# Add and GELU on one core: HBM blocks dealt to partitions in a different order

## Chip, cores and metric

The kernel runs on one core of one Trainium2 chip. The metric is device time in microseconds (us), from three runs before the change. The profile is one execution of the program, recorded by the hardware profiler; its times count from the first instruction.

## What is computed

Two float32 matrices of 1024 x 4096 are added, and the tanh form of GELU is applied to each element of the sum:

```python
def reference(x, y):                      # both float32 [1024, 4096]
    z = x + y
    return (0.5 * z * (1 + np.tanh(np.sqrt(2 / np.pi) * (z + 0.044715 * z ** 3)))).astype(np.float32)
```

Each input and the output has 16.78 MB, so 33.55 MB are read from HBM (the chip's main memory) and 16.78 MB written. Nothing is reused: each element is read once, worked on and written once.

## The kernel before

SBUF, the on-chip memory, has 128 partitions. Each of the three HBM tensors is seen as 128 blocks of 8 rows, a block being 32768 contiguous elements or 128 KB. Block p belongs to partition p. The views `xv`, `yv` and `ov` express this in one line (L93):

```python
xv, yv, ov = (a.rearrange("(p n) d -> p (n d)", p=P) for a in (x, y, out))
```

A tile `z` holds all 32768 elements of every partition. x is loaded straight into it, y into one of two buffers of 8192 elements per partition, and the sum goes back into `z`, as does the result. Columns are cut in three ways:

- loads: four pieces of 8192 columns, each of x (`load_x`, L128) and of y (`load_y`, L135). A load piece is 32 KB in each partition, 4.19 MB in all.
- computing: sixteen chunks of 2048 columns.
- stores: three pieces of 16384, 10240 and 6144 columns (`store`, L139).

For each chunk, GpSimd (POOL in the profile) adds y to x (`add`, L152; chunk 0 is added by VectorE, DVE); ScalarE (ACT) squares with a scale into a PSUM tile (`sq`, L157); VectorE forms (w + c1) * z (`stt`, L163); ScalarE takes the sigmoid (`sig`, L168); and VectorE multiplies it by z, back into `z` (`mul`, L175). The form z * sigmoid(...) equals the tanh form.

The order on each engine's queue is written out by hand at the end of the function. SyncE (SP) issues all eleven transfers on one queue: x0, y0, x1, y1, x2, y2, x3, y3, then the three stores. The issue of y2 waits until the adds on y0 are done, since they share a buffer, and y3 likewise for y1. The first store is made to wait for the first half of the multiply of chunk 9 (`FIRST`), so that it joins the queue when the loads are nearly through. Two helpers work on the compiled program: `begin_early` moves the first two loads ahead of the program's opening barrier, and `wait_late` moves the wait for the last store behind the closing barrier. The transfer hardware has 16 DMA engines; one transfer is spread over them.

## Time and profile before

| | |
|---|---|
| median of three runs | 120.35 us (120.22 to 120.42) |
| the profiled execution: its time | 120.44 us |
| the profiled execution: span, first to last instruction | 118.8 us |
| DMA queue, share of 16 engines over the span | 98.8% |
| read and written | 33.55 MB and 16.78 MB, 424 GB/s on average |
| DVE, POOL, ACT busy | 73.7, 69.6 and 61.0 us |
| x load, issue to landing (median of four) | 31.4 us |
| y load, issue to landing (median of four) | 22.2 us |
| the three stores, issue to landing | 22.0, 15.8 and 11.9 us |

The time is measured from outside and is 1.6 us longer than the span. "Busy" counts an engine's own instructions; the rest of its span it waits. For transfers, time from issue to landing includes waiting behind earlier transfers of the queue. The page also divides the span into 40 equal slices and gives, for each, an engine's busy share as a digit in tenths, the mean share of the 16 DMA engines, and the GB/s moved. A packet is what one DMA engine moves in one go.

### The profile page before, as it was taken

Reading aid. Unit: us, or ns where it says so; the run is one execution under the profiler, and the core shown is the slowest. Engines: PE = TensorE matmul, PEld = TensorE weight load, DVE = VectorE, ACT = ScalarE, POOL = GpSimd, SP = SyncE. Lnnn points to the kernel's source line nnn. Section 1 sums busy time; section 2 is a strip of 40 time slices with the busy share of each in tenths; the row PEclk is TensorE's granted clock in tenths of the full one; section 3 lists DMA queues with packets and bytes.
Section 4 is the critical chain, followed back from the end, with each engine's and each line's share of the span. In section 5 each row is a group of like instructions: output and inputs, shape, how many; then the busy total and the mean of one; then the engine's idle time right before and its main releaser. Section 6 shows DMA issues by size and latency. Waiting matters only on the chain.

```text
span 118.8 us, 172 instructions
## 1 busy us (share of the span) xinstructions
DVE 73.7 (62%) x35; ACT 61.0 (51%) x34; POOL 69.6 (59%) x19
## 2 busy tenths in 40 slices
DVE  0000000635799995739999968999994999990000
ACT  5000000063888965197698647888839779810000
POOL 0000000699996099999959999959999990000000
DMA  7989898989999898989899898998899889999996
GB/s 243 463 386 497 353 530 353 508 375 475 408 419 463 375 508 353 519 364 508 375 430 452 386 497 353 519 541 353 353 596 463 353 353 441 441 441 441 389 406 265
DMA packets 1584, 50.33 MB, mean 424 GB/s; under 512 B 176, under 2 KB 176, under 8 KB 176
## 3 DMA queue, kind: packets, MB, share of 16 engines
q1 hardware_dynamic: 1584, 50.33, 98.8%
HBM read 33.55 MB, written 16.78 MB: 424 GB/s over the span
## 4 chain that ended last, share of the span: by engine, by line
DMA 51%; POOL 26%; POOLq 4%; DVE 4%; DVEq 2%; ACT 2%; issue 0%; SPq 0%
DMA y<-in_y_dram 51%; POOL z L152 26%; POOLq L230 4%; DVE w L163 2%; DVEq L230 2%; DVE z L175 2%; ACT w L157 2%; SPq L128 0%; POOLq L152 0%
## 5 line engine op out<-in xcount | busy, mean ns | idle before, releaser
L152 POOL TENSOR_TENSOR z<-z,y 128x2048 f32<-128x2048 f32 x15 | 69.4, 4658 | 28.3 <-DMA y<-in_y_dram 28.3
L157 ACT ACTIVATE w<-z 128x2048 f32<-128x2048 f32 x16 | 30.1, 1882 | 37.7 <-DVE z L152 21.5
L163 DVE SCALAR_TENSOR_TENSOR w<-w,z 128x2048 f32<-128x2048 f32 x16 | 36.7, 2296 | 11.3 <-ACT w L157 11.1
L175 DVE TENSOR_TENSOR z<-w,z 128x2048 f32<-128x2048 f32 (+1 forms) x17 | 35.9, 2155 | 0.0
L168 ACT ACTIVATE w<-w 128x2048 f32<-128x2048 f32 x16 | 29.7, 1855 | 4.4 <-DVE w L163 4.3
L152 DVE TENSOR_TENSOR z<-z,y 128x2048 f32<-128x2048 f32 x1 | 2.3, 2291 | 20.5 <-DMA y<-in_y_dram 20.5
L215 ACT ACT_TABLE_LOAD x1 | 1.3, 1283 | 1.3 <-PEq L247 1.3
L214 DVE MEMSET one<- 128x1 f32 x1 | 0.1, 59 | 1.3 <-PEq L247 1.3
L247 POOL MEMSET const-float32-0.0<- 128x1 f32 x1 | 0.1, 99 | 0.2 <-issue 0.2
L215 ACT ACTIVATE one<-one 128x1 f32<-128x1 f32 x1 | 0.2, 203 | 0.0
L247 POOL MEMSET const-bfloat16-1.0<- 128x1 bf16 x1 | 0.1, 101 | 0.0
L247 POOL MEMSET const-uint8-127<- 128x1 uint8 x1 | 0.1, 101 | 0.0
L247 POOL MEMSET const-float32-1.0<- 128x1 f32 x1 | 0.1, 98 | 0.0
## 6 DMA issues: line engine op xcount, KB each, us to landing
z<-in_x_dram SPq DMA_DIRECT2D x4, 4096.0 KB, 31.4
y<-in_y_dram SPq DMA_DIRECT2D x4, 4096.0 KB, 22.2
out_dram<-z SPq DMA_DIRECT2D x1, 5120.0 KB, 15.8
out_dram<-z SPq DMA_DIRECT2D x1, 3072.0 KB, 11.9
out_dram<-z SPq DMA_DIRECT2D x1, 22.0
```

Of the source, the lines that this page charges most:

```text
L152: eng.tensor_add(out=zt[:, a:b], in0=zt[:, a:b], in1=yt[s][:, o : o + b - a])
L157: nc.scalar.activation(out=wt[c], in_=zt[:, a:b], func=act.Square, scale=root)
L163: nc.vector.scalar_tensor_tensor(out=wt[c], in0=wt[c], scalar=c1, in1=zt[:, a:b], op0=alu.add, op1=alu.mult)
L168: nc.scalar.activation(out=wt[c], in_=wt[c], func=act.Sigmoid)
L175: ins = nc.vector.tensor_mul(out=zt[:, a + o : a + o + n], in0=wt[c][:, o : o + n], in1=zt[:, a + o : a + o + n],)
L214: nc.vector.memset(one, 0.0)
L215: nc.scalar.activation(out=one, in_=one, func=act.Sigmoid)
L230: tc.compile()
L247: nc = _bacc.Bacc("TRN2", target_bir_lowering=False, num_devices=1)
```

## The change

The views of x, y and the output get another order. The 128 blocks are numbered 16*j + e, with e from 0 to 15 and j from 0 to 7, and the views become three-dimensional: e first, then j, then the 32768 contiguous elements of a block. Against an SBUF tile of 128 partitions, taken in order, block 16*j + e goes to partition 8*e + j. The loads and the stores use the same view, so an element is written where it was read. [...]

```diff
-    xv, yv, ov = (a.rearrange("(p n) d -> p (n d)", p=P) for a in (x, y, out))
+    xv, yv, ov = (
+        a.rearrange("(j e n) d -> e j (n d)", j=8, e=16) for a in (x, y, out)
+    )
...
-        nc.sync.dma_start(out=zt[:, a:b], in_=xv[:, a:b])
+        nc.sync.dma_start(out=zt[:, a:b], in_=xv[:, :, a:b])
...
-        nc.sync.dma_start(out=yt[s][:, o : o + b - a], in_=yv[:, a:b])
+        nc.sync.dma_start(out=yt[s][:, o : o + b - a], in_=yv[:, :, a:b])
...
-        ins = nc.sync.dma_start(out=ov[:, a:b], in_=zt[:, a:b])
+        ins = nc.sync.dma_start(out=ov[:, :, a:b], in_=zt[:, a:b])
```

Nothing else differs: sizes, tiles, waits and the order of all queues stay.

## Prediction

> **What bounds the kernel now.** I read the page from the top: busy engines first, then the transfers, then the chain.

> ```profile
> span 118.8 us, 172 instructions
> DVE 73.7 (62%) x35; ACT 61.0 (51%) x34; POOL 69.6 (59%) x19
> ...
> DMA  7989898989999898989899898998899889999996
> ...
> q1 hardware_dynamic: 1584, 50.33, 98.8%
> HBM read 33.55 MB, written 16.78 MB: 424 GB/s over the span
> ```

> No computing engine is busy for more than 62% of the span. The single transfer queue occupies the 16 DMA engines for 98.8% of it, 117.4 us each, and its row of tenths never falls between the first slice and the last. So 118.8 us is 117.4 us of transfers plus 1.4 us around them; the first instruction issues a load at 0.00, and its first data packet starts 1.0 us later.

> The chain that ended last seems to say something else:

> ```profile
> DMA 51%; POOL 26%; POOLq 4%; DVE 4%; DVEq 2%; ACT 2%; issue 0%; SPq 0%
> ```

> It leads through the last y load (landed at 80.1) into the adds and multiplies that precede the last store, issued at 106.9. But that store takes 11.9 us to land, and its 3.15 MB need only 3.15 MB / 435 GB/s = 7.2 us. For 4.7 us it stood behind the store before it. The computing chain has 4.7 us of slack at the end; the transfers have none.

> Next, how fast each engine goes. Over two stretches (columns: length, DVE, ACT, POOL, clock, DMA share, GB/s):

> ```profile
> 20.00:40.00 20.00, 14.01 (x7) 11.72 (x7) 15.58 (x3) 1.00 1.00 431
> 40.00:60.00 20.00, 16.16 (x8) 13.10 (x8) 17.93 (x4) 1.00 1.02 437
> ```

> 431 to 437 GB/s over 16 engines is 27 GB/s each, also in the stores: the trace's packet records give 1213 ns for a 32 KB load packet (27.0 GB/s) and 912 ns for a 24 KB store packet (26.9). A packet is one partition's contiguous run. All 1024 load packets take 1211 to 1238 ns, except the first sixteen, at 1.69 to 2.20 us. Summed over all packets and divided by 16, the excess over 1213 ns per 32 KB is **0.77 us**: 0.67 in those first packets, 0.12 in the other loads, -0.02 in the stores. That is all that a kinder order of HBM addresses can win once transfers run.

> Last, how the engines stand to each other. The same queue in 40 slices of 0.3 us, from 40 to 52 us:

> ```profile
> DMA  0990099009900990099009900990099009920992
> GB/s 0 1311 437 0 0 1201 546 0 0 1092 655 0 0 983 765 0 0 874 874 0 0 874 874 0 0 765 983 0 0 655 1092 0 0 655 983 109 0 655 983 109
> ```

> Packets are counted where they start. Every fourth slice comes round again: the 16 engines begin their packets together, each 1.2 us. One such round in the packet records starts between 41.53 and 42.01, a spread of 0.48 us or 0.4 of a packet; the round from 100.03 to 100.49 has the same. The engines march in step from end to end.

> [...]

> **The change, part by part.** Sizes, tiles, instruction counts, queue order, waits and the number of 32 KB runs stay. All that moves is which HBM block goes to which partition: block p before, block 16*(p mod 8) + p // 8 after. Loads and the store share the map, so the elementwise work is untouched and no engine's instruction changes.

> (1) *HBM order.* [...] Gain: between 0 and 0.77 us, the whole excess above. [...] I take 0: [...] at today's order the trace shows no loss after the first round.

> (2) *The issue.* The HBM side gets a second counting dimension (16, 8) against one of 128 in SBUF. An issue takes 0.33 to 0.49 us; only the first one is ahead of all data. I bound this by 0 to +0.4 us (a doubling) and take 0; the other ten are issued while earlier transfers hold the engines.

> (3) *Who carries which partition.* This decides. Slowest counts are now 16 in HBM and 128 in SBUF. [...]

> The same from the trace: if a pair shares equally with no lead, every packet takes twice 1213 ns and 117.4 us becomes 234.8. A lead of L packets survives sharing, since both advance alike, and saves it for L of every four: four packets then cost 8 - L packet times. The spread seen, at most 0.4, gives 7.6/4 = 1.9, or 223 us; the pair with the least lead ends last, so I stay nearer to 2. I take 231. Stores read SBUF by the same map; if reading did not collide, only the loads (33.55 MB, 78 us) would double: 117.4 + 78 = 195. The bound below is no effect at all[...].

> What becomes late: nothing in computing. At half rate a 4.19 MB load takes 19 us instead of 9.7; x0 to x2 and y0, y1 queue 94 us of work, while the third y load waits only for adds on y0 (done some 16 us after it lands at about 40). Loads end near 157; the last chunk's multiply follows within the 27 us seen before (80.1 to 106.9), near 184, while the first store holds the engines to about 195. All waits lie beside transfers.

> Sum for the profiled execution: 1.4 + 231 + 0 + 0 = 232.4 us of span; its own time stood 120.44 to a span of 118.8, so 1.6 more: 234.0. The runs' median is 0.1 lower than the profiled time. Forecast **234 us**, 1.94 times before.

> **Rivals.** A measurement here can tell 0.2%, about 0.24 us, from no change.

> A, *pairs drift apart*: [...] Or only loads collide. Against it: leads in the trace stay the same from 41 to 100 us, though under no contention. Price: from 122 to 215; the loads-only case 195 + 3.0 = 198.

> B, *not slower[...]*. [...] no packet gets longer, and only the order in HBM differs. [...] Time: 120.4, within 0.2% if the first packets stay slow; if the dense order cures them, down to 120.35 - 0.77 = 119.6. [...]

> C, *HBM pitch*: [...]

> **How the numbers follow.** Lock-step collision (215 to 240): 0.60. A: 0.15. C, or a small loss from the longer issue: 0.06. B unchanged: 0.12; B with the first packets cured: 0.07. So faster 0.07, same 0.12, slower 0.81. The range reaches from the middle of B's unchanged case, 120.3, to 240, just above the full doubling with what lies around it (234.8 + 3.0 = 237.8).

> **What would show it.** Right: 32 KB packets near 2.4 us, about 218 GB/s in every stretch of loads and stores, transfers at 98% or more of a doubled span, POOL and DVE idle mostly on y loads, first y landing near 40 us. Step 3 is wrong if load packets stay at 1.21 us; the half of it on stores if stores run at 435 GB/s; equal sharing if rates climb with time or the rounds of packets lose step. [...] The whole is wrong if the page repeats 424 GB/s.

## The result: 1.94 times the time before

The changed kernel takes **233.59 us** (median of six runs, 232.45 to 234.89), against 120.41 us for the kernel before (six runs, 120.22 to 120.84): 1.9389 times, 95% interval 1.9317 to 1.9462. The forecast was 234 us. The profiled execution took 233.56 us, with a span of 231.9.

The page after, the same lines as were read before:

```profile
span 231.9 us, 172 instructions
DVE 73.9 (32%) x35; ACT 61.0 (26%) x34; POOL 69.6 (30%) x19
...
DMA  8998998998998998998999999899989998999892
GB/s 192 215 226 187 220 226 181 215 237 181 215 237 181 198 254 181 198 254 181 198 220 215 192 220 220 181 226 317 362 181 215 203 226 220 219 254 212 252 280 89
...
q1 hardware_dynamic: 1584, 50.33, 98.0%
HBM read 33.55 MB, written 16.78 MB: 217 GB/s over the span
```

Instructions, busy times, packets and bytes are those of before. The DMA engines are as busy as before, 98.0% of the span, and move half as much per microsecond. So a share of busy time says nothing on the rate: a packet that takes twice as long is counted as busy twice as long.

The queue in 40 slices of 0.3 us, from 40 to 52 us, as shown for before:

```profile
DMA  0094999000999990000999900009599900009999
GB/s 0 0 218 109 328 765 328 0 0 0 218 218 437 655 218 0 0 0 0 328 218 437 765 0 0 0 0 218 109 546 655 218 0 0 0 0 328 328 328 765
DMA packets 96, 2.62 MB, mean 218 GB/s; under 512 B 16, under 2 KB 16, under 8 KB 16
```

The rounds of sixteen packets still come together, but every eighth slice instead of every fourth. In the packet records a 32 KB load packet takes 2.50 us on average where it took 1.225; in a row of four, three take about 2.56 and one 2.36.

Who waited for whom (total, times, longest), first before, then after:

```profile
POOL z L152 <- DMA y<-in_y_dram: 28.3, 4, 21.5
```

```profile
POOL z L154 <- DMA y<-in_y_dram: 111.0, 4, 42.5
ACT w L159 <- POOL z L154: 76.2, 11, 22.8
DVE w L165 <- ACT w L159: 72.4, 8, 22.2
DVE z L154 <- DMA y<-in_y_dram: 40.8, 1, 40.8
```

GpSimd waits for y, ScalarE for GpSimd and VectorE for ScalarE: the idle time that was added to computing goes back to the loads.

### The profile page after: what moved, and what is told of

It reads as the page before. It is cut to its first block, busy times and chain, and to the rows that moved or that the text cites. A ratio compares the mean times of both kernels' runs of the same rounds, so it can differ in the third digit from the quotient of the medians.

```text
span 231.9 us, 172 instructions
## 1 busy us (share of the span) xinstructions
DVE 73.9 (32%) x35; ACT 61.0 (26%) x34; POOL 69.6 (30%) x19
## 2 busy tenths in 40 slices
DMA packets 1584, 50.33 MB, mean 217 GB/s; under 512 B 176, under 2 KB 176, under 8 KB 176
## 3 DMA queue, kind: packets, MB, share of 16 engines
q1 hardware_dynamic: 1584, 50.33, 98.0%
HBM read 33.55 MB, written 16.78 MB: 217 GB/s over the span
## 4 chain that ended last, share of the span: by engine, by line
another core or an unknown queue 29%; POOL 28%; DMA 18%; POOLq 2%; DVE 2%; DVEq 1%; ACT 1%; SPq 0%; issue 0%
POOL z L154 28%; DMA y<-in_y_dram 18%; POOLq L232 2%; DVE w L165 1%; DVEq L232 1%; DVE z L177 1%; ACT w L159 1%; SPq L130 0%; POOLq L154 0%
```

## Experiments

**1. The issue alone.** Transfers on which both sides count along one dimension carry a mark in the program (`ant_dge_precooked`) that those of the changed kernel lack. Here the kernel before loses it, and each side gets a dummy dimension:

```diff
+ new = [[s, n], [1, 1], inner]            # both sides, still 128 against 128
...
+ block.instructions[k] = i.__replace__(**sides, ant_dge_precooked=False)
```

> The kernel before, with its own order of blocks; every transfer only loses the mark in the program that gives it the short issue path, and gets a dummy dimension of size 1 on both sides, so that it is issued as the changed kernel's transfers are, still 128 against 128. Port theory (engines collide where the split runs along a dimension of 16): 120.4 to 120.8 us, packets of 1.21 us, issues 0.5 to 0.7 us. Issue-path rival (it is the loss of the short path that spoils the spread): about 234 us.

Measured: 120.81 us, 1.0021 times before (1.0012 to 1.0031). The first issue grew from 0.38 to 0.58 us and the first data packet starts at 1.37 us instead of 1.01; load packets stay at 1.21. The issue costs some 0.25 us, not 113. The rival that the issue costs the time is out.

**2. The split alone.** Block p stays in partition p, so no address changes; only the HBM side is counted as 16 by 8:

```diff
+ new = [[s * n // e, e], [s, n // e], inner]      # HBM side, n = 128, e = 16
...
+ new = [[s, n], [1, 1], inner]                    # SBUF side
```

> The block order of before (block p to partition p), but the HBM side counted as 16 by 8 (steps 1 MB and 128 KB) against 128 partitions. The addresses are those of before, only the split can change. Port theory: 225 to 240 us, load packets 2.4 to 2.6 us. HBM-order rival (the new order of addresses costs the time): 120 to 121 us.

Measured: 231.76 us. From its page:

```profile
span 230.1 us, 172 instructions
...
HBM read 33.55 MB, written 16.78 MB: 219 GB/s over the span
```

The same bytes from the same addresses to the same partitions take, within 1%, as long as in the changed kernel. Which block lies in which partition has no part in it; how the transfer is counted makes the difference. One thing is left open here: the split may also decide which addresses are read at the same moment. Experiment 6 comes back to this.

**3. The change with 32 by 4.**

```diff
-        a.rearrange("(j e n) d -> e j (n d)", j=8, e=16) for a in (x, y, out)
+        a.rearrange("(j e n) d -> e j (n d)", j=4, e=32) for a in (x, y, out)
```

> The changed kernel with 32 by 4 instead of 16 by 8: block 32*j + e to partition 4*e + j. Neighbouring blocks 128 KB apart still go to neighbouring groups of partitions. [...] Port theory: 120 to 121 us[...], 225 to 240 us[...]. HBM-order rival: well above 121 us in both cases, since the order is as dense as in the changed kernel.

Measured: 120.91 us, 1.0033 times before (1.002 to 1.0045).

```profile
span 119.2 us, 172 instructions
...
HBM read 33.55 MB, written 16.78 MB: 422 GB/s over the span
```

Load packets are back at 1.21 us. A map as dense as that of the change, with neighbouring blocks side by side, costs 0.1 us more than experiment 1 (120.81), which has the order of before and also lacks the mark; it wins nothing. The sixteen first packets, slow before (an excess of 0.67 us, as summed in the prediction), have 0.55 here. How the 32 groups of blocks are dealt to the engines, on which the theory's two times turn, no trace shows; the rate of 422 GB/s says only that packets don't lengthen each other here.

**4 and 5. Loads alone, stores alone.** The edit of experiment 2, made for the eight loads or for the three stores only.

> The block order of before; the eight loads counted as 16 by 8, the three stores as 128. Port theory: loads as in the changed kernel (about 162 us until the last y lands), then 16.78 MB of stores at 435 GB/s (38.5 us): 200 to 206 us. If the stores never collide even with a split by 16, stores would be as fast in the changed kernel, where they took 69 us: so 231 us or more would say that the loads set it all.

> The block order of before; loads counted as 128, the three stores as 16 by 8. Port theory: loads end near 80 us as before, then stores at the changed kernel's 242 GB/s (69 us) or at a full half (77 us): 150 to 160 us. If reads of SBUF don't collide at a port: 120 to 122 us.

Measured: 202.77 us with the loads, 157.6 with the stores. In stretches divided where the last y load has landed (length, DVE, ACT, POOL, clock, DMA share, GB/s), loads alone:

```profile
1.40:162.70 161.30, 56.05 (x27) 46.13 (x26) 51.40 (x11) 1.00 1.01 215
162.70:201.10 38.40, 17.88 (x8) 14.88 (x8) 17.93 (x4) 1.00 0.95 410
```

and stores alone:

```profile
1.00:80.00 79.00, 48.62 (x24) 41.79 (x24) 51.48 (x11) 1.00 1.05 438
80.00:155.90 75.90, 25.12 (x12) 19.22 (x11) 17.95 (x4) 1.00 0.89 207
```

Each part is slow where it is split by 16 (215 and 207 GB/s) and fast where it isn't (438 and 410). (A window that opens as packets begin counts some of them early, so 215 in loads is a little high: 33.55 MB from 1.4 to 161.9 us are 209.) Packets that read SBUF lengthen too, though less evenly: store packets range from full speed (1.21) to 2.9 us per 32 KB.

**6. The ports by themselves.** The kernel before, with three extra x loads one after the other in front:

```diff
+    def phase(i):   # x8, x4: x with j = 8 or 4, as "(j e n) d -> e j (n d)"
+        src, e, rows = ((x8, 4, 32), (x4, 8, 32), (x8, 8, 64))[i]
+        nc.sync.dma_start(out=zt[:rows, :8192], in_=src[:e, :, :8192])
```

> The kernel before, with three extra x loads ahead of its own, one after the other, each into the first 8192 columns; their data is overwritten by the first real load. First, 4 by 8 blocks into partitions 0-31 (four engines, eight partitions each); second, 8 by 4 into the same 32 partitions (eight engines, four each[...]); third, 8 by 8 into partitions 0-63 (eight engines, eight each[...]). Port theory: 105 to 109 GB/s, then 210 to 218, then again 100 to 109, with packets of 1.21, 1.21 and 2.4 to 2.6 us. If an engine is slow by itself when it serves eight neighbouring partitions, the first is slow too (2.4 us, 54 GB/s). If eight engines are slow by number or by a second counting dimension, the second is slow too. After these, 1.0 + 118.8 us as before: 165 to 175 us in all.

Measured: 162.78 us in all, just below the 165 to 175 expected; the three rates came as the port theory has them. One stretch within each extra load (same columns):

```profile
4.40:9.25 4.85, 0.00 (x0) 0.00 (x0) 0.00 (x0) 1.00 0.25 108
15.40:17.85 2.45, 0.00 (x0) 0.00 (x0) 0.00 (x0) 1.00 0.49 214
23.40:36.20 12.80, 0.00 (x0) 0.00 (x0) 0.00 (x0) 1.00 0.50 105
```

Four engines (a DMA share of 0.25) into partitions 0-31 give 108 GB/s, with packets of 1.21 us. Eight engines with four partitions each, **in the same 32 partitions**, give 214, again at 1.21. The same number of engines over *twice* the partitions, eight each, gives 105, with packets mostly of 2.56. The DMA share is equal in the last two. An engine isn't slow because it serves eight partitions (first) nor because of eight engines or two counting dimensions (second): it is slow, 2.56 us a packet and not 1.21, when others load into the other 32 partitions beside it. On what experiment 2 left open it gives a hint: if each engine takes its share in order, which is the author's estimate, the second and the third load both read blocks 0 to 7 first, and only the third is slow: HBM addresses in step would then not be the cause. Of the experiments, this and the second decide the case.

**7. A head start.** The prediction held that a lead within a pair survives. The base is the changed kernel with four stores of 8192 columns:

> The changed kernel with four stores of 8192 columns, each gated by its own chunks only (and by chunk 7), so that all packets have 32 KB. It is the base for the two runs with a head start. Port theory: 230 to 240 us, no gain, as the engines still go in step.

Measured: 231.02 us, as expected. Then dummy loads ahead of it, on some engines only:

```diff
+    def delay(n):                          # in the second run 4096, not 8192
+        at = {12: 0, 4: 12}[n]
+        nc.sync.dma_start(out=zt[at : at + n, TOT - 8192 :], in_=xd[:n, :8192])
+    sp = [(delay, 12), (delay, 4)]         # ahead of the loads
```

> As the run before, with two dummy loads ahead of all others, of 12 and of 4 rows[...]; their data is overwritten by the last x load. Port theory with equal sharing: [...] packets fall to 1.21 us after the delay and the time to 128 to 138 us, in spite of 0.5 MB more traffic[...]. If an engine is slow for any reason of its own[...]: 235 to 245 us.

> The same with dummies of half the size, about two packet times of lead. Port theory with equal sharing: four packets take 8 - 2 = 6 packet times, 117 x 1.5 = 176 us, plus 5 us of dummies and 3 around: 175 to 190 us. If leads are pulled together by the sharing: towards 235; if they are driven apart: towards 130.

Measured: 226.28 and 227.56 us. Both expectations missed: four load packets together fell only from 10.07 us in the base to 9.89 in the first and 9.97 in the second. The next run asked why, with four dummies of four rows:

```diff
+    def delay(i):
+        n = (12288, 128, 10240, 128)[i]
+        nc.sync.dma_start(out=zt[4*i : 4*i + 4, TOT - n :], in_=xd[4*i : 4*i + 4, :n])
```

> The head start again, since the two runs before seem to have given none: there all engines showed one dummy packet of 3 to 4 us, as if the dummy of four rows had gone to the four engines that the dummy of twelve left out. Here four dummies of four rows each: 48 KB, 512 B, 40 KB, 512 B per row. If each dummy takes the next four engines, [...] load packets fall below 1.7 us and the time to 128 to 170 us. If all four go to engines 0 to 3, [...] half of the early load packets get short, and the time stays at 220 to 235 us. If a lead is lost in the sharing itself, packets grow back to 2.5 us within the first two loads and the time is 225 to 235 us.

Measured: 233.9 us. The time fits two of the cases named, but no load packets became short: from 17.4 us on they take 2.36 to 2.56. The guess of the text above, that dummies go to engines left free, is refuted: in the packet records the first dummy's four packets end between 6.9 and 7.7 us, and only then, one by one, do the second's and the third's begin: the same four engines. Which four, the records do not show.

But the records hold something else. While these four loaded 40 KB each into four neighbouring partitions (8 to 11) in 6.83 us, 6.0 GB/s each and 24 together, less than one engine alone (27.0), **all the other twelve** moved 32 KB in 5.33 us (6.1 GB/s). In these loads all sixteen engines go at about one rate, also in the changed kernel, where the shorter packet of four (2.36 us) comes in the same round on all of them. In stores they do not: after 194 us there, packets of 1.51 and of 2.9 us for 40 KB run side by side. Why the twelve were slow too no run shows.

So a delay in time gives no lead of that length: counted in bytes, the first of the two runs above had sixteen dummy packets in all, which by the author's estimate put one engine of a pair one packet ahead, not four. A lead has to be counted in bytes. Here 76 packets of 32 KB come first, meant to put one engine of each pair about four ahead:

```diff
+    def delay(k):
+        at, j = {12: (0, 5), 4: (60, 4)}[k]   # 12 x 5 rows, then 4 x 4
+        nc.sync.dma_start(
+            out=zt[at : at + k * j, TOT - 8192 :], in_=xv[:k, :j, TOT - 8192 :])
```

> In the run before, [...] the other twelve also moved only 32 KB in 5.3 us: all sixteen go at about one rate, so a head start is to be counted in bytes. [...] If pairs collide only while both are on one port and leads last: load packets of 1.2 to 1.6 us after the first 20 us, 135 to 165 us in all. If a lead is lost in the common rate, or collisions do not depend on the phase: load packets stay at 2.3 to 2.6 us and the time at 230 to 250 us.

Measured: **157.3 us**, with 2.5 MB more to load; 135 to 165 were expected. Its slices, 3.9 us each, and one stretch of loads:

```profile
GB/s 135 236 227 177 236 185 379 379 429 404 379 370 446 395 370 395 446 387 387 387 446 379 387 395 437 387 471 412 404 421 471 446 345 236 219 151 269 202 227 109
```

```profile
20.00:60.00 40.00, 10.15 (x5) 8.37 (x5) 14.12 (x3) 1.00 0.99 379
```

After the dummies (to about 23 us) the rate is near 400 GB/s (404 from 25 to 61 us), with the addresses and the split of the changed kernel. Of four load packets two take 1.22 us, one 1.27 and one 1.52 to 1.57; the stores up to 131 us keep to 1.21 for the most part. Then engines run out of work, since the last store waits for its multiply (issued near 135); all start it together, and most packets are back at 2.5 us. So the collision is a matter of phase: the same loads took 10.07 us for four packets in the base, with all engines in step, and take 5.23 here.

## Why the prediction was right

*What bounds.* Right: transfers alone set the span, so longer packets lengthened it one for one.

*HBM order, taken as 0.* Right, by experiment 2 and by 3 against 1, and by 6 as far as the author's estimate there holds. Rival C, that steps of 2 MB from block to block in HBM cost the time, is out: the last run of experiment 7 has the 2 MB steps of the change with packets of 1.22 us, and experiment 2 is slow with steps of 128 KB.

*Issue, taken as 0 within 0 to 0.4 us.* It costs: the first issue takes 0.67 us, the first data starts at 1.44 instead of 1.01, and experiment 1 prices it at 0.25 us of the time. It lay ahead of all data, as said, and inside the bound.

*Who carries which partition.* Right in what can be measured: the count of 16 lengthens packets. Experiment 2 takes 231.76 us with every block in its old partition, and in experiment 6 eight engines need 2.56 us a packet over 64 partitions and 1.21 over 32. Which engine carries which partitions, and where two of them meet, was the author's estimate and was not shown. Rival B, that no packet gets longer, falls: load packets went from 1.225 to 2.50 us on average.

*The size, 231 us.* Three errors cancel. By the packet records an engine's transfers in the profiled execution sum to 227.2 us, 160.3 in loads and 66.9 in stores; half of the rate before (437 GB/s from 40 to 60 us), 218, gives 153.9 and 77.0. So the rate was not 218 in every stretch, as the prediction said, but 209 in loads and 237 in stores. Loads are slower because two engines together get less than one: two packets of 32 KB in 2.56 us are 25.6 GB/s, where one alone had 27.0. In stores the engines fall out of step, and some packets run at full speed (40 KB in 1.51 us). The 12 us from 200 us on, in slices of 0.3 us, show no rounds any more:

```profile
DMA  6909069969790470397096999895909696996660
```

The 1.4 us around the transfers became 4.7: the later first packet, and engines that end at different times, between about 228 and 231.5 us. 160.3 + 66.9 + 4.7 = 231.9, against 232.4 forecast. That the sum comes so close is luck; that packets lengthen each other, and the factor near two, are what it got right.

*The lead.* That a lead survives in loads is right (7), and so is its arithmetic at that lead if 2.56 us stands for a packet in step: four take 4 x 2.56 - L x (2.56 - 1.21); the 5.23 us of the last run give L = 3.7, where about four were meant. At a lead of one packet the sum gives 8.89, where the first head start, with one packet by the author's estimate, took 9.89; so it is shown for the long lead alone. Wrong was the notion that each pair has its own pace and the least lead only ends last: in loads all engines keep one pace (6.0 and 6.1 GB/s in the fourth run of experiment 7). Rival A, pairs that drift apart, did not occur in loads; in stores the engines did fall out of step (40 KB in 1.51 us beside 2.9). Its other form, that only loads collide, is refuted by experiment 5.

*What becomes late.* Right: the last load packet ended at 161.9 us (said: near 157), the last multiply at 189.4 (near 184), and the first store held the engines to 196.6 (about 195). No computing wait reached the end. Two slips in the working change nothing: five loads of 19.2 us are 96 us of work, not 94, and the round given as 100.03 to 100.49 begins at 99.97.

## What to carry to other kernels

The shape of the HBM side of a transfer, not only its bytes and partitions, decides its rate: with 128 SBUF partitions, a slowest dimension of 16 about halved it (217 and 219 GB/s over the span, from 424), and 32 kept it (422), as did 128 (120.81 us in experiment 1); 64 was not tried. Look at the time of one packet and at the GB/s of a stretch, not at the DMA share, which was 98 to 99% in both kernels. Before rearranging addresses, sum what packets lose against their best; here that sum was 0.77 us, and the one dense order that kept the rate (experiment 3) won nothing.

## What was not expected

- In the loads of the changed kernel two engines get 25.6 GB/s together (2.56 us for a packet of each), 5% less than one alone (27.0).
- While four engines loaded into four neighbouring partitions, all sixteen were slow: 6.0 GB/s for each of the four, 6.1 for each of the twelve others (experiment 7).
- The first two store packets in the changed kernel run at or near full speed: 2.55 to 2.67 and then 2.42 us for 64 KB, on all engines, before most take 4.4 to 5.4. Slices of 317 and 362 GB/s on its page are these. In the run with the stores alone split by 16 there is no such burst. Why was not tested.
